# FFN of a hybrid decoder layer: the scales of a chunk's up and down weights from one chain, and the samples' parts of h from one instruction each

## The chip, the cores and the metric

The kernel runs on one core of one Trainium2 chip. The time is that of the device for one execution, in microseconds. The engines work side by side, each on its own queue in order: TensorE (PE, with its weight loads PEld), VectorE (DVE), ScalarE (ACT), GpSimd (POOL), and SyncE (SP), which here issues the DMA transfers.

## What is computed

One layer of a decoder trunk for 2048 prompt tokens and 32 sample tokens (8 samples of 4), width 1024. A mixing part (state space models, attention, a short convolution) comes first; the change leaves its instructions as they are. It is followed by the FFN:

```python
hn = rmsnorm(x, P['norm_ffn_g'][l])
x = x + jnp.square(jax.nn.relu(hn @ P['w_up'][l])) @ P['w_down'][l]
```

`w_up` is 1024 x 4096, `w_down` 4096 x 1024, all in float32; the prompt and the samples share the weights.

## The kernel before

**Numbers.** TensorE is fed with float16. Each float32 operand is split into a high part and a low part (`split`, L174: ScalarE writes the high part, VectorE the low one), and each product is made of three matmuls. So that weights fit the range of float16, a set of weights is multiplied by a power of two. `wscale` (L179) finds it: ScalarE squares the set and sums it by row (L183; the squares go to a junk place), a product with a matrix of ones sums over the partitions (through `mm`, L140), VectorE bounds it from below (L187), GpSimd raises it to the power -1/2 (L188), VectorE masks out the mantissa (`pow2`, L155), multiplies (L191) and takes the reciprocal (L192). This is a chain over four engines on a single column, 128 x 1.

**Tiling.** The FFN's width of 4096 is cut into 16 chunks of 256 columns (`FC`). The prompt is worked in two passes, s = 0 and s = 1, of two blocks of 512 tokens; the samples ride along with the first block of pass 0, so that its up products have 272 columns where the others have 256. In each pass all 16 chunks are loaded (1 MB of `w_up`, 1 MB of `w_down`) and split again. The scales are found in pass 0 alone and kept in `wsc` for pass 1.

**Both products use seven products for eight** (a Strassen-like scheme): GpSimd makes sums and differences of quarters of the up weights (L2036 to L2039), of the down weights (L2062 to L2065) and of h (L2138 to L2149). Chunk 15 takes the plain eight-product form for the down product.

**One chunk.** `ffn_wu` (L2019) loads the up weights, finds their scale in pass 0, and writes the split weights `wu`. `ffn_wd` (L2044) does the same for the down weights and writes `wd` and `wdT`. `up` (L2079) makes h for one block: seven products, ScalarE and VectorE add them up in the tile `fr` (four quarters, `C`), ScalarE applies relu and square, and then h is split into `ht`. In the first block of pass 0 the 16 sample columns of each quarter are also split, into `hs` (L2128 on ScalarE, L2129 on VectorE): four copies and four subtractions a chunk. `down` (L2154) multiplies h with the down weights and adds the result to the residual `x` (L2191, VectorE, one addition of 512 columns for each step); the samples' product comes first, 32 matmuls into a bank of its own, added to `accs` (L2166).

**The loop** (L2222 on) goes through steps (s, c, b), and each step issues in the program: `up` of the next step, then the weights of the next chunk (`ffn_wu` in the first block's step, `ffn_wd` in the second's), then `down` of this step.

**What sets the order.** The program order gives each instruction a priority; a planner in the tile framework, with a model of the engines' times, puts the instructions on the engines' queues and adds the waits. It takes a ready instruction of lower priority where one of higher priority isn't ready. So up and down products are interleaved on TensorE, and a change in one place can shift the planned order around it.

**Buffers.** The loaded weights (`ws`) have two buffers, used in turn by up and down weights: a load of down weights starts when the split of the chunk before has read the down weights for the last time (the wdT split, L177). `wu` has two buffers, `wd` and `wdT` share four. In PSUM, the tag `w` of the ones product uses the single bank `d`, which the samples' product uses too; down products and most of the up products rotate through five banks `b`, which come free when VectorE or ScalarE has read them.

Of the kernel before, what the change touches and what calls it, by code (L numbers as in the profile page):

```python
# [99 lines left out]
def dram(ap, offset, dims):  # L100
    return bass.AP(tensor=ap.tensor, offset=ap.offset + offset, ap=[list(d) for d in dims])


class K:
# [58 lines left out]
    def wprep(self, loads, kt, ncols, tag="w", st=None):  # L163


        nc = self.nc
        st = self.wload(loads, kt, ncols, tag) if st is None else st
        w = self.wp.tile([128, kt, 2, ncols], F16, name="w", tag=tag, bufs=None if tag == "w" else 1)
        sc, inv = self.col("w_sc", bufs=12), self.col("w_inv", bufs=12)
        self.wscale(st, w[:, :, 0, :], sc, inv, 15)  # L170
        self.split(w[:, :, 0, :], w[:, :, 1, :], st, sc)
        return w, sc, inv
# [5 lines left out]

    def wscale(self, st, junk, sc, inv, top):  # L179

        nc = self.nc
        ss = self.col("w_ss", bufs=4)
        nc.scalar.activation(junk, st, AF.Square, accum_out=ss)  # L183
        p = self.ps("w", [128, 512])
        self.mm(p[:, :1], self.ones, ss)
        f = self.col("w_f", bufs=4)
        nc.vector.tensor_scalar(f, p[:, :1], 1e-12, None, op0=OP.max)  # L187
        nc.gpsimd.tensor_tensor(f, f, self.mhalf[:, :1], op=OP.pow)  # L188
        m = self.col("w_m", bufs=4)
        self.pow2(m, f)  # L190
        nc.vector.tensor_scalar(sc, m, float(2 ** top), None, op0=OP.mult)  # L191
        nc.vector.reciprocal(inv, sc)  # L192
# [1684 lines left out]
    def outproj(self, ctx, mix):  # L1877
# [50 lines left out]
        self.accs = self.hp.tile([128, 8, NS], F32, name="accs")  # L1928
        self.wsc = self.hp.tile([128, 2, 4096 // FC, 2], F32, name="wsc")
        self.x2, self.hn = {}, {}  # L1930
# [52 lines left out]
    def out_sample(self, hn, g8):  # L1983
# [27 lines left out]
        for t in range(2):  # L2011
            for i in range(2):
                nc.vector.tensor_mul(xt[:, i, t], sq[:, :, 16 * t + 8 * i:16 * t + 8 * i + 8],
                                     g8[:, :, None].to_broadcast([128, 8, 8]))
# [28 lines left out]

    def ffn_wd(self, s, c):  # L2044


        nc, A = self.nc, self.A
        st = self.wload(lambda st: [(st, dram(A["w_down"], c * FC * D, [[D, 128], [128 * D, FC // 128], [1, D]]))], FC // 128, D)
        w = self.wp.tile([128, FC // 128, 2, D], F16, name="wd", tag="w")
        sc, inv = self.wsc[:, 1, c, 0:1], self.wsc[:, 1, c, 1:2]  # L2050
        if s == 0:
            self.wscale(st, w[:, :, 0, :], sc, inv, 14)
        if s == 0 or (s, c) in PLAIN:
# [16 lines left out]
    def ffn(self):  # L2070
# [8 lines left out]
        def up(s, c, b):  # L2079
# [29 lines left out]
            prod(r, 1, 1)  # L2109
            add(0, r, 0)  # L2110
            prod(p, 6, 3, False)
# [3 lines left out]
            prod(p, 4, 2, False)  # L2115
            nc.scalar.activation(C[:, 2, :], p[:, :N], AF.Relu, scale=RS)
            for i in range(4):
                x = C[:, i, :]
                if i != 2:
# [17 lines left out]
            A11, A22, A21, A12 = (C[:, i, :] for i in range(4))  # L2137
            nc.gpsimd.tensor_add(S[:, 0, :], A21, A22)  # L2138
# [6 lines left out]
            nc.scalar.activation(ht[:, 0:2, 0, :], C[:, 0:2, :], AF.Copy)  # L2145
            nc.gpsimd.tensor_sub(ht[:, 0:2, 1, :], C[:, 0:2, :], ht[:, 0:2, 0, :])  # L2146
            nc.scalar.activation(ht[:, 2, 0, :], A12, AF.Copy)
# [5 lines left out]
        def down(s, c, b, ht, f):  # L2153
# [26 lines left out]
        def down_pair(wd, wt, x2, ht, f):  # L2180
# [11 lines left out]
            p, q, r = (self.ps("mm", [128, 512]) for _ in range(3))  # L2192
            prod(p, 0, "11")
            add(0, 0, p)
# [5 lines left out]
            add(1, 0, p)  # L2200
            prod(q, 1, "T4", False)
            add(1, 0, q)
# [5 lines left out]
        def down_plain(wd, x2, ht, f):  # L2208
            for t, parts in enumerate(((0, 3), (2, 1))):
                for h in range(2):  # L2210
# [94 lines left out]
```

## Time and profile before

| what | value |
|---|---|
| median of 3 runs | 2594.95 us |
| lowest and highest | 2593.56 and 2594.98 us |
| profiled execution, its own time | 2598.28 us |
| span of that execution in the trace | 2596.5 us |
| TensorE busy | 2439.7 us (94%) |
| VectorE busy | 2010.8 us (77%) |
| ScalarE busy | 1313.2 us (51%) |
| GpSimd busy | 1212.3 us (47%) |

The FFN takes about the second half of the span: pass 0 from about 1300 us to 1957 us, pass 1 from there to the end. Busy shares are over the whole span; a stage has its own. The granted clock of TensorE is given as a share of full speed, and it is at full speed in the stretches shown below.

### The profile page before, as it was taken

Reading aid. Unit: us, or ns where it says so; the run is one execution under the profiler, and the core shown is the slowest. Engines: PE = TensorE matmul, PEld = TensorE weight load, DVE = VectorE, ACT = ScalarE, POOL = GpSimd, SP = SyncE. Lnnn points to the kernel's source line nnn. Section 1 sums busy time; section 2 is a strip of 40 time slices with the busy share of each in tenths; the row PEclk is TensorE's granted clock in tenths of the full one; section 3 lists DMA queues with packets and bytes.
Section 4 is the critical chain, followed back from the end, with each engine's and each line's share of the span. In section 5 each row is a group of like instructions: output and inputs, shape, how many; then the busy total and the mean of one; then the engine's idle time right before and its main releaser. Section 6 shows DMA issues by size and latency. Waiting matters only on the chain.

```text
span 2596.5 us, 51309 instructions
## 1 busy us (share of the span) xinstructions
PE 2439.7 (94%) x20496; PEld 1663.5 (64%) x20496; DVE 2010.8 (77%) x3746; ACT 1313.2 (51%) x2449; POOL 1212.3 (47%) x1265
## 2 busy tenths in 40 slices
PE   7989999999999899999979999999998999999997
PEld 6975554454467677689856666666665666666664
DVE  7566667874576777654589998889997898999996
ACT  6534332033346677562455555665556454555554
POOL 3403122223114566550255555656556665666652
PEclk9989999999999998999979999999999999999999
DMA  6333416879632433356111111111135211121201
GB/s 176 102 81 86 99 30 218 302 248 334 224 101 77 136 96 104 101 171 216 52 41 50 51 64 50 49 66 34 62 124 214 74 62 49 53 66 49 66 33 65
DMA packets 209321, 277.78 MB, mean 107 GB/s; under 512 B 42837, under 2 KB 177106, under 8 KB 198810
## 3 DMA queue, kind: packets, MB, share of 16 engines
q1 hardware_dynamic: 195050, 202.65, 25.0%
q0 software_dynamic: 9376, 67.64, 7.2%
q10 hardware_dynamic: 4656, 4.23, 0.5%
q8 instruction: 160, 2.62, 0.4%
q14 instruction: 79, 0.65, 0.1%
HBM read 217.33 MB, written 54.29 MB: 105 GB/s over the span
## 4 chain that ended last, share of the span: by engine, by line
PE 51%; DVE 16%; POOL 13%; DMA 6%; ACT 6%; issue 5%; SPq 1%; POOLq 0%; DVEq 0%; ACTq 0%
PE pb L140 25%; PE px L140 23%; DVE x L2191 4%; DVE wu L177 2%; PE pd L140 2%; DMA kp<-in_cache_v_dram,ptV 1%; DVE wd L177 1%; PE pb L144 1%; POOL ht L2146 1%; POOL ws L2037 1%; POOL ht L2148 1%; DVE wdT L177 1%; POOL ws L2039 1%; POOL ws L2038 1%; POOL ws L2036 1%
## 5 line engine op out<-in xcount | busy, mean ns | idle before, releaser
L140 PEld LDWEIGHTS <-wu 128*128 128x128 f16 x5376 | 530.3, 99 | 222.9 <-issue 37.3
L2191 DVE SCALAR_TENSOR_TENSOR x<-pb,ff,x 128x512 f32<-128x512 f32 x840 | 591.3, 740 | 27.3 <-PE pb L140 23.3
L140 PE MATMUL px<-hn,wu 128*128 128x256 f16 (+1 forms) x3072 | 428.0, 276 | 14.6 <-DVE hn L1981 7.0
L140 PEld LDWEIGHTS <-ht 128*128 128x128 f16 x2712 | 264.5, 99 | 231.6 <-issue 26.0
L140 PE MATMUL pb<-wdT,ht 128*128 128x512 f16 x1440 | 379.8, 381 | 15.8 <-DVE x L2191 9.2
L140 PE MATMUL px<-xT,w 128*128 128x512 f16 (+1 forms) x1968 | 371.9, 341 | 1.5 <-ACT da L731 1.2
L140 PE MATMUL pb<-wd,ht 128*128 128x512 f16 x1272 | 336.8, 381 | 6.1 <-DVE x L2191 5.2
L140 PE MATMUL pb<-hn,wu 128*128 128x256 f16 (+1 forms) x2304 | 303.6, 277 | 15.8 <-DVE x L2191 7.6
L140 PEld LDWEIGHTS <-w 128*128 128x128 f16 x2160 | 168.6, 99 | 188.1 <-issue 30.9
L909 POOL TENSOR_TENSOR pl<-P,ph 128x512 f16<-128x512 f32 (+3 forms) x160 | 166.9, 1053 | 155.5 <-ACT ph L906 59.6
L176 ACT ACTIVATE wu<-ws,wsc 128x1024 f16<-128x1024 f32 (+1 forms) x128 | 129.4, 1036 | 130.8 <-POOL ws L2039 76.7
L140 PE MATMUL px<-w,cat 128*128 128x256 f16 x1536 | 180.2, 274 | 3.4 <-DMA cat<-cat 3.3
L177 DVE SCALAR_TENSOR_TENSOR wu<-ws,wsc,wu 128x1024 f16<-128x1024 f32 (+1 forms) x128 | 168.6, 1331 | 18.0 <-ACT wu L176 17.7
L140 PEld LDWEIGHTS <-cat 128*128 128x128 f16 x1536 | 149.6, 98 | 25.7 <-DMA cat<-cat 3.4
L140 PE MATMUL px<-w,xT 128*128 128x128 f16 (+1 forms) x2400 | 156.1, 225 | 10.2 <-DVE v L576 4.5
L140 PEld LDWEIGHTS <-xT 128*128 128x128 f16 (+1 forms) x2672 | 153.1, 101 | 15.5 <-issue 5.5
L902 ACT ACTIVATE P<-pb,nck,cc 128x512 f32<-128x512 f32 (+3 forms) x160 | 112.2, 710 | 75.4 <-PE pb L140 69.7
L2143 ACT ACTIVATE ht<-fr 128x1024 f16<-128x1024 f32 (+1 forms) x60 | 64.2, 1070 | 159.9 <-POOL fr L2149 159.9
L2146 POOL TENSOR_TENSOR ht<-fr,ht 128x512 f16<-128x512 f32 (+1 forms) x60 | 84.2, 1403 | 113.0 <-ACT ht L2145 113.0
L2062 POOL TENSOR_TENSOR ws<-ws 128x512 f32<-128x512 f32 x30 | 41.1, 1371 | 187.1 <-DVE wd L177 187.1
L871 DVE TENSOR_REDUCE mx<-pb 128x1 f32<-128x512 f32 (+3 forms) x160 | 94.8, 607 | 40.0 <-PE pb L140 38.9
L2120 ACT ACTIVATE fr<-fr 128x256 f32<-128x256 f32 (+1 forms) x192 | 77.0, 414 | 90.5 <-DVE fr L2101 89.7
(717 smaller groups left out, 4647.1 us busy)
## 6 DMA issues: line engine op xcount, KB each, us to landing
ws<-in_w_up_dram SPq DMA_DIRECT2D x32, 1024.0 KB
ws<-in_w_down_dram SPq DMA_DIRECT2D x32, 1024.0 KB
ws<-in_w_in_dram SPq DMA_DIRECT2D x22, 512.0 KB
x<-in_x_prompt_dram SPq DMA_DIRECT2D x16, 512.0 KB
cat<-cat SPq DMA_DIRECT2D x32, 256.0 KB
x<-in_x_prompt_dram SPq DMA_DIRECT2D x8, 1024.0 KB
out_y_prompt_dram<-x SPq DMA_DIRECT2D x32, 256.0 KB
hnD<-hnr SPq DMA_DIRECT2D x4, 1792.0 KB
```

The costliest lines, as they stand in the source:

```text
L140: self.nc.tensor.matmul(out, lhsT, rhs, start=start, stop=stop, skip_group_check=True)
L144: self.nc.tensor.transpose(out, in_, self.ident[:n, :n])
L176: self.nc.scalar.activation(hi, x, AF.Copy, scale=sc)
L177: self.nc.vector.scalar_tensor_tensor(lo, x, sc, hi, op0=OP.mult, op1=OP.subtract)
L871: nc.vector.tensor_reduce(mx[:, ii, jb:jb + 1], s[:, :n], axis=AX.X, op=OP.max)
L902: nc.scalar.activation(P[:, :n], s[:, :n], AF.Exp, bias=nck[:, j, h, kt:kt + 1], scale=cc[:, h // 2:h // 2 + 1])
L909: (nc.gpsimd if 1 else nc.vector).tensor_sub(pl[:, :n], P[:, :n], ph[:, :n])
L2062: nc.gpsimd.tensor_sub(B11, B12, B11)
L2120: nc.scalar.activation(x, x, AF.Relu)
L2143: nc.scalar.activation(ht[:, o:o + m, 0, :], x, AF.Copy)
L2146: nc.gpsimd.tensor_sub(ht[:, 0:2, 1, :], C[:, 0:2, :], ht[:, 0:2, 0, :])
L2191: nc.vector.scalar_tensor_tensor(o, p, f, o, op0=OP.mult, op1=OP.add)
```

## The change

1. `wscale` takes a list of weight sets and works on as many columns. For chunks 1 to 15 in pass 0, `ffn_wu` now loads the down weights as well (`wd_load`, kept in `wst_down` until `ffn_wd` takes them), squares both sets, and one chain finds both scales on two columns. The two sets of squares go to different parts of the `wu` tile. Chunk 0 keeps two chains of one column. `wsc` has its axes in another order, so that the two scales of a chunk stand side by side.
2. The samples' columns of all four quarters of h are copied by one ScalarE instruction and subtracted by one VectorE instruction, into a tile `hs` with its axes in another order (parts, t, m, i, n). For this the quarters stand in another order in `C`, and what indexes them is changed with it: the additions, the order of squares, the operands of the down products, and the order of the samples' halves in `out_sample`.
3. The samples' product reads `hs` through an access pattern with more axes (runs of 16 columns), with the same number of matmuls and columns.

```diff
     def wscale(self, sts, sc, inv, top):
-        nc = self.nc
-        ss = self.col("w_ss", bufs=4)
-        nc.scalar.activation(junk, st, AF.Square, accum_out=ss)
+        nc, n = self.nc, len(sts)
+        ss = self.col(f"w_ss{n}", w=n, bufs=4)
+        for k, (st, junk) in enumerate(sts):
+            nc.scalar.activation(junk, st, AF.Square, accum_out=ss[:, k:k + 1])
         p = self.ps("w", [128, 512])
-        self.mm(p[:, :1], self.ones, ss)
-        f = self.col("w_f", bufs=4)
-        nc.vector.tensor_scalar(f, p[:, :1], 1e-12, None, op0=OP.max)
-        nc.gpsimd.tensor_tensor(f, f, self.mhalf[:, :1], op=OP.pow)
-        m = self.col("w_m", bufs=4)
+        self.mm(p[:, :n], self.ones, ss)
+        f = self.col(f"w_f{n}", w=n, bufs=4)
+        nc.vector.tensor_scalar(f, p[:, :n], 1e-12, None, op0=OP.max)
+        nc.gpsimd.tensor_tensor(f, f, self.mhalf[:, :n], op=OP.pow)
+        m = self.col(f"w_m{n}", w=n, bufs=4)
...
     def ffn_wu(self, s, c):
-        sc, inv = self.wsc[:, 0, c, 0:1], self.wsc[:, 0, c, 1:2]
+        sc, inv = self.wsc[:, c, 0, 0:1], self.wsc[:, c, 1, 0:1]
         if s == 0:
-            self.wscale(st, w[:, 3:7].rearrange("p o k a n -> p (o k a n)")[:, :KT * FC].rearrange("p (k n) -> p k n", n=FC),
-                        sc, inv, 14)
+            flat = w.rearrange("p o k a n -> p (o k a n)")
+            sts = [(st, flat[:, 3072:5120].rearrange("p (k n) -> p k n", n=FC))]
+            if c:
+                self.wst_down[c] = self.wd_load(c)
+                sts.append((self.wst_down[c], flat[:, 5120:7168].rearrange("p (k n) -> p k n", n=D)))
+            n = len(sts)
+            self.wscale(sts, self.wsc[:, c, 0, :n], self.wsc[:, c, 1, :n], 14)
...
+    def wd_load(self, c):
+        A = self.A["w_down"]
+        return self.wload(lambda st: [(st, dram(A, c * FC * D, [[D, 128], [128 * D, FC // 128], [1, D]]))], FC // 128, D)
+
     def ffn_wd(self, s, c):
-        st = self.wload(lambda st: [(st, dram(A["w_down"], c * FC * D, [[D, 128], [128 * D, FC // 128], [1, D]]))], FC // 128, D)
+        st = self.wst_down.pop(c, None) or self.wd_load(c)
         w = self.wp.tile([128, FC // 128, 2, D], F16, name="wd", tag="w")
-        if s == 0:
-            self.wscale(st, w[:, :, 0, :], sc, inv, 14)
+        if (s, c) == (0, 0):
+            self.wscale([(st, w[:, :, 0, :])], sc, inv, 14)
...
         def up(s, c, b):
...
                 hs = self.hp.tile([128, 2, 2, 2, 2, 8], F16, name="hs", bufs=2)
-                for m in range(2):
-                    for t in range(2):
-                        x = C[:, ((0, 2), (3, 1))[m][t], :].rearrange("p (i n) -> p i n", i=2)[:, :, 128:]
-                        nc.scalar.activation(hs[:, m, 0, t], x, AF.Copy)
-                        nc.vector.tensor_sub(hs[:, m, 1, t], x, hs[:, m, 0, t])
+                x = C.rearrange("p c (i n) -> p c i n", i=2)[:, :, :, 128:]
+                hh, hl = (hs[:, a].rearrange("p t m i n -> p (t m) i n") for a in range(2))
+                nc.scalar.activation(hh, x, AF.Copy)
+                nc.vector.tensor_sub(hl, x, hh)
...
         def down(s, c, b, ht, f):
...
-                        x, o = hs[:, k].rearrange("p a t i n -> p (a t i n)"), p[:, m].rearrange("p a n -> p (a n)")
+                        x, o = hs[:, :, :, k], p[:, m].rearrange("p a (t i n) -> p a t i n", t=2, i=2)
                         self.mm(o, wd[:, k, 0, m * 128:(m + 1) * 128], x, start=m + k == 0, stop=False)
-                        self.mm(o[:, 0:NS], wd[:, k, 1, m * 128:(m + 1) * 128], x[:, 0:NS], start=False, stop=k == 1)
+                        self.mm(o[:, 0], wd[:, k, 1, m * 128:(m + 1) * 128], x[:, 0], start=False, stop=k == 1)
```

## Rows read from the trace of the kernel before

**Rows 1.** the page's engine totals: busy us, share, instructions

```profile
PE 2439.7 (94%) x20496; PEld 1663.5 (64%) x20496; DVE 2010.8 (77%) x3746; ACT 1313.2 (51%) x2449; POOL 1212.3 (47%) x1265
```

**Rows 2.** engines by stretch, pass 0 then pass 1: us, busy per engine, clock, DMA

```profile
1410.24:1896.02 485.78, 466.61 (x3474) 312.63 (x3472) 440.64 (x711) 285.43 (x504) 282.73 (x265) 1.00 0.16 53
2203.35:2497.05 293.70, 293.57 (x2019) 197.30 (x2018) 276.54 (x366) 152.12 (x281) 186.78 (x162) 1.00 0.18 58
```

**Rows 3.** waits in pass 0 (1342 to 1957): total us, times, longest

```profile
PE pb L140 <- DVE x L2191: 20.2, 19, 4.4
DVE w_m L155 <- POOL w_f L188: 9.5, 9, 1.6
DVE hs L2129 <- ACT hs L2128: 6.8, 10, 3.3
```

**Rows 4.** timeline of a stall: start, us, engine, line, [idle <-releaser]

```profile
1610.01 2.35 DVE L177 SCALAR_TENSOR_TENSOR wdT<-ws,wsc,wdT 128x2048 f16<-128x2048 f32 x1 [0.41 <-ACT wdT L176]
1612.28 1.27 DVE L2129 TENSOR_TENSOR hs<-fr,hs 128x16 f16<-128x16 f32 x2
1614.13 0.73 DVE L2129 TENSOR_TENSOR hs<-fr,hs 128x16 f16<-128x16 f32 x1
1614.26 0.81 PE L140 MATMUL pb<-wdT,ht 128*128 128x512 f16 x3 [2.27 <-DVE x L2191]
```

**Rows 5.** VectorE's groups in pass 0: count, busy us, mean ns, idle before

```profile
L2129 DVE TENSOR_TENSOR hs<-fr,hs 128x16 f16<-128x16 f32 x60 | 32.5, 548 | 6.8 <-ACT hs L2128 6.8
L155 DVE TENSOR_SCALAR w_m<-w_f 128x1 int32<-128x1 int32 x29 | 4.2, 146 | 9.6 <-POOL w_f L188 9.5
```

**Rows 6.** timeline, an hs subtraction and the GpSimd operation before it

```profile
1525.93 1.26 POOL L2065 TENSOR_TENSOR ws<-ws 128x512 f32<-128x512 f32 x1
1526.10 1.13 DVE L2129 TENSOR_TENSOR hs<-fr,hs 128x16 f16<-128x16 f32 x1 [0.55 <-ACT hs L2128]
```

**Rows 7.** nearest sizes: VectorE's groups of the whole run; GpSimd's power on 32 columns

```profile
L1981 DVE TENSOR_TENSOR hn<-os,hn 128x128 f16<-128x128 f32 x2 | 0.5, 282 | 0.0
1260.52 5.82 POOL L2007 TENSOR_TENSOR os_rs<-os_rs,mhalf 128x32 f32<-128x32 f32 x1 [4.01 <-DVE os_rs L2006]
```

**Rows 8.** timeline, the sample product's first matmuls of that chunk

```profile
1623.41 0.92 PE L140 MATMUL pd<-hs,wd 128*128 128x64 f16 x28
```

**Rows 9.** timeline, loads, squares, ones products and scales of one chunk

```profile
1595.95 0.37 SPq L160 DMA_DIRECT2D ws<-in_w_up_dram  x1
1602.70 1.91 ACT L183 ACTIVATE wu<-ws 128x2048 f16<-128x2048 f32 x1 [3.83 <-DMA ws<-in_w_up_dram]
...
1611.71 0.28 PE L140 MATMUL pd<-w_ss,ones 128*128 128x1 f32 x2
1612.38 0.37 SPq L160 DMA_DIRECT2D ws<-in_w_down_dram  x1
1620.06 0.14 DVE L191 TENSOR_SCALAR wsc<-w_m 128x1 f32<-128x1 f32 x1
...
1632.52 0.37 SPq L160 DMA_DIRECT2D ws<-in_w_up_dram  x1
1633.23 0.28 PE L140 MATMUL pd<-w_ss,ones 128*128 128x1 f32 x2
1635.84 0.55 POOL L188 TENSOR_TENSOR w_f<-w_f,mhalf 128x1 f32<-128x1 f32 x1
1638.86 0.14 DVE L191 TENSOR_SCALAR wsc<-w_m 128x1 f32<-128x1 f32 x1
1640.21 1.99 ACT L176 ACTIVATE wd<-ws,wsc 128x2048 f16<-128x2048 f32 x1
...
1654.44 0.37 SPq L160 DMA_DIRECT2D ws<-in_w_down_dram  x1
```

**Rows 10.** timeline, chunk 1, both scales at hand together

```profile
1348.28 0.15 DVE L191 TENSOR_SCALAR wsc<-w_m 128x1 f32<-128x1 f32 x1
...
1372.35 0.37 SPq L160 DMA_DIRECT2D ws<-in_w_down_dram  x1
```

More of the change, by code (lines that the diff above doesn't have):

```diff
@@ L169, in wprep @@
         sc, inv = self.col("w_sc", bufs=12), self.col("w_inv", bufs=12)
-        self.wscale(st, w[:, :, 0, :], sc, inv, 15)
+        self.wscale([(st, w[:, :, 0, :])], sc, inv, 15)
         self.split(w[:, :, 0, :], w[:, :, 1, :], st, sc)
@@ L177, in split, with wscale @@
         self.nc.vector.scalar_tensor_tensor(lo, x, sc, hi, op0=OP.mult, op1=OP.subtract)
-    def wscale(self, st, junk, sc, inv, top):
-        nc = self.nc
-        ss = self.col("w_ss", bufs=4)
-        nc.scalar.activation(junk, st, AF.Square, accum_out=ss)
-        p = self.ps("w", [128, 512])
-        self.mm(p[:, :1], self.ones, ss)
-        f = self.col("w_f", bufs=4)
-        nc.vector.tensor_scalar(f, p[:, :1], 1e-12, None, op0=OP.max)
-        nc.gpsimd.tensor_tensor(f, f, self.mhalf[:, :1], op=OP.pow)
-        m = self.col("w_m", bufs=4)
+    def wscale(self, sts, sc, inv, top):
+        nc, n = self.nc, len(sts)
+        ss = self.col(f"w_ss{n}", w=n, bufs=4)
+        for k, (st, junk) in enumerate(sts):
+            nc.scalar.activation(junk, st, AF.Square, accum_out=ss[:, k:k + 1])
+        p = self.ps("w", [128, 512])
+        self.mm(p[:, :n], self.ones, ss)
[3 more added lines that the diff above has]
+        m = self.col(f"w_m{n}", w=n, bufs=4)
         self.pow2(m, f)
@@ L1928, in outproj @@
         self.accs = self.hp.tile([128, 8, NS], F32, name="accs")
-        self.wsc = self.hp.tile([128, 2, 4096 // FC, 2], F32, name="wsc")
+        self.wsc = self.hp.tile([128, 4096 // FC, 2, 2], F32, name="wsc")
+        self.wst_down = {}
         self.x2, self.hn = {}, {}
@@ L2012, in out_sample @@
             for i in range(2):
-                nc.vector.tensor_mul(xt[:, i, t], sq[:, :, 16 * t + 8 * i:16 * t + 8 * i + 8],
+                nc.vector.tensor_mul(xt[:, i, 1 - t], sq[:, :, 16 * t + 8 * i:16 * t + 8 * i + 8],
                                      g8[:, :, None].to_broadcast([128, 8, 8]))
@@ L2042, in ffn_wu @@
         self.wts[s, c] = w, inv
+    def wd_load(self, c):
+        A = self.A["w_down"]
+        return self.wload(lambda st: [(st, dram(A, c * FC * D, [[D, 128], [128 * D, FC // 128], [1, D]]))], FC // 128, D)
     def ffn_wd(self, s, c):
-        nc, A = self.nc, self.A
-        st = self.wload(lambda st: [(st, dram(A["w_down"], c * FC * D, [[D, 128], [128 * D, FC // 128], [1, D]]))], FC // 128, D)
+        nc = self.nc
+        st = self.wst_down.pop(c, None) or self.wd_load(c)
         w = self.wp.tile([128, FC // 128, 2, D], F16, name="wd", tag="w")
-        sc, inv = self.wsc[:, 1, c, 0:1], self.wsc[:, 1, c, 1:2]
-        if s == 0:
-            self.wscale(st, w[:, :, 0, :], sc, inv, 14)
+        sc, inv = self.wsc[:, c, 0, 1:2], self.wsc[:, c, 1, 1:2]
+        if (s, c) == (0, 0):
+            self.wscale([(st, w[:, :, 0, :])], sc, inv, 14)
         if s == 0 or (s, c) in PLAIN:
@@ L2109, in up @@
             prod(r, 1, 1)
-            add(0, r, 0)
+            add(2, r, 0)
             prod(p, 6, 3, False)
@@ L2115, in up @@
             prod(p, 4, 2, False)
-            nc.scalar.activation(C[:, 2, :], p[:, :N], AF.Relu, scale=RS)
-            for i in range(4):
+            nc.scalar.activation(C[:, 0, :], p[:, :N], AF.Relu, scale=RS)
+            for i in (2, 1, 0, 3):
                 x = C[:, i, :]
-                if i != 2:
+                if i:
                     nc.scalar.activation(x, x, AF.Relu)
@@ L2136, in up @@
                 return ht, hs
-            A11, A22, A21, A12 = (C[:, i, :] for i in range(4))
+            A21, A22, A11, A12 = (C[:, i, :] for i in range(4))
             nc.gpsimd.tensor_add(S[:, 0, :], A21, A22)
@@ L2144, in parts @@
                 nc.vector.tensor_sub(ht[:, o:o + m, 1, :], x, ht[:, o:o + m, 0, :])
-            nc.scalar.activation(ht[:, 0:2, 0, :], C[:, 0:2, :], AF.Copy)
-            nc.gpsimd.tensor_sub(ht[:, 0:2, 1, :], C[:, 0:2, :], ht[:, 0:2, 0, :])
+            nc.scalar.activation(ht[:, 0:2, 0, :], C[:, 1:3, :], AF.Copy)
+            nc.gpsimd.tensor_sub(ht[:, 0:2, 1, :], C[:, 1:3, :], ht[:, 0:2, 0, :])
             nc.scalar.activation(ht[:, 2, 0, :], A12, AF.Copy)
@@ L2192, in down_pair @@
             p, q, r = (self.ps("mm", [128, 512]) for _ in range(3))
-            prod(p, 0, "11")
+            prod(p, 1, "11")
             add(0, 0, p)
@@ L2200, in down_pair @@
             add(1, 0, p)
-            prod(q, 1, "T4", False)
+            prod(q, 0, "T4", False)
             add(1, 0, q)
@@ L2208, in down_plain @@
         def down_plain(wd, x2, ht, f):
-            for t, parts in enumerate(((0, 3), (2, 1))):
+            for t, parts in enumerate(((2, 3), (0, 1))):
                 for h in range(2):
```

## The prediction

> **What bounds the kernel now.** I read first the page's engine totals: TensorE is busy 94% of the span [rows 1], so the change can only pay where TensorE stands still, or where it removes TensorE work. Then I cut the span by stage. The change touches only pass 0 of the FFN (scales are found there alone, and only its first block carries the samples), so I compared a steady stretch of pass 0 with one of pass 1 [rows 2]. The first holds 12 chunks in 485.78 us, 40.48 us each; the second, eight chunks in 293.70 us, 36.71 us each. In pass 1 TensorE never stops (293.57 of 293.70 busy), though VectorE is busy 94% there. In pass 0 TensorE is busy 38.88 us of each 40.48 and VectorE 91%. So VectorE's load alone does not stall TensorE; something in pass 0 makes it late at the wrong moments. About 15 chunks run like this, so TensorE's idle time there is some 15 x 1.60 = 24 us, and that is nearly all there is to win.
>
> The view of waits says who ends that idle time: 20.2 us of it is a down product waiting for VectorE to add an earlier one to the residual (L2191), so that a PSUM bank comes free [rows 3]. The timeline of one such place shows why VectorE was late [rows 4]: it finished the 2.35 us split of wdT, then did two of the small subtractions for hs (1.27 us for both), and only then the addition that let TensorE go on after 2.27 us; the next thing on VectorE was another hs, 0.73 us. I went through all stalls of this kind: in 14 of the 19, together 18 us, an hs subtraction stands within the few VectorE instructions just ahead.
>
> **The change part by part.**
> *The samples' parts.* Four subtractions per chunk become one. There are 60 in the FFN of pass 0, 548 ns in the mean for 16 columns [rows 5]. That price is not their work. The rows show the reason: a subtraction that began at 1526.10 while GpSimd was inside an operation ended at 1527.23, and that operation ended at 1527.19 [rows 6]. The work alone is small: a subtraction of 128 columns took 282 ns [rows 7]. The merged one has 64 columns, so it should take under 282 ns unblocked, and once in a while a GpSimd operation more; I take the same 548 ns. VectorE then loses 45 x 0.548 = 24.7 us of busy time and about three quarters of the 6.8 us it waits for ScalarE's copies [rows 3]. If the price went instead with the columns, one merged subtraction would cost 4 x 0.548 = 2.2 us and nothing would be saved; against that stands that subtractions of the same 16 columns took 0.73 us at one place [rows 4] and 1.13 us at another [rows 6]. The Trainium skill ("SBUF — State Buffer", Who interferes with whom) says that a VectorE instruction with two SBUF inputs and a GpSimd instruction that reads SBUF exclude each other for the whole of the earlier one; by that rule too the price is paid per instruction, and the saving is the 24.7 us, not zero. ScalarE's four copies become one; it is busy 59% of this stretch [rows 2] and this costs or gives nothing on the path. The merged pair must wait for the last of the four quarters of h. Its reader, the sample product, needs all four today too, and came at 1623.41 [rows 8], 8.5 us after the hs subtraction that began at 1614.13 had ended [rows 4]; that gap hides the wait. Were it gone, at most the price of one subtraction, 0.7 us there, would be added in each chunk.
>
> What reaches TensorE: of the 18 us of stalls with an hs subtraction ahead, I take half, 9 us. The reason for half is that a typical stall has one or two of these in the queue ahead (0.55 to 1.3 us), and its mean is 18/14 = 1.3 us, the rest being the wdT split and the additions. Bounds 0 and 18 us.
>
> *One chain instead of two.* For chunks 1 to 15 one of the two chains of ones product, max, power, mask, multiplication and reciprocal goes. On TensorE that is two passes, 0.28 us in the timeline [rows 9], 15 x 0.28 = 4.2 us; this lies on the engine that sets the end, so it counts in full. On VectorE four operations of about 146 ns [rows 5] go, 15 x 0.58 = 8.8 us, and about half of the 9.5 us that it waits for GpSimd's power [rows 3]. The power itself takes 5.82 us for 32 columns [rows 7] against 0.55 us for one (1635.84, [rows 9]), about 170 ns a column, so the two-column one costs about 0.72 us, less than two. I give VectorE's relief here no price of its own beyond the 9 us above; with it, at most all of the 24 us idle time goes.
>
> *The new wait.* The scale of the up weights now also needs the down weights' load and its sum of squares. Program order puts that load just behind the up load on SP's queue; both are already issued when their buffer comes free, in turn, so the queue itself gains nothing behind it. What waits is the chain. Today in one chunk [rows 9]: the down load is issued at 1612.38 (its buffer is read for the last time by the wdT split), the ones product of the up weights has just run at 1611.71, and their scale is there at 1620.06, 7.7 us after the down load's issue. A load takes about 6.7 us (issued 1595.95, ScalarE's square started at 1602.70 having waited 3.83 us for it), the square 1.9 us, the accumulator read 0.2 us; from ones product to scale there are 5.6 us (1633.23 to 1638.86) or 8.4 us (1611.71 to 1620.06). So the common scale comes 14.4 to 17.2 us after the down load's issue, the up weights are split 7 to 10 us later than now, but the down weights' scale comes some 9 to 12 us earlier than its 1638.86. While it waits, the square holds up ScalarE's copies out of PSUM, and the ones product holds up every product queued behind it on TensorE.
>
> Is that covered? The down buffer makes a loop: load, square, chain, splits of both, next load. Chunk 1 is the nearest row for the splits with both scales at hand: from the first of the two scales at 1348.28 to the next down load at 1372.35, 24.1 us [rows 10]. With 24.1 the loop is 14.4 + 24.1 = 38.5 us at the better chain, 41.3 us at the worse. TensorE's own work will be 38.88 - 0.28 = 38.6 us a chunk. So the loop lies just at TensorE's floor at the better end and passes today's 40.48 us at the worse. I take it as covered, at no cost, because the up split's late start is followed by an early down split, and TensorE has both blocks' down products to do meanwhile; but with no room to spare.
>
> **Sum.** 4.2 + 9 = 13 us off the profiled execution's 2598.28 us (span 2596.5 and 1.8 around it), 2585 us. The median of the three runs is 3.3 us lower, 2594.95, so I forecast 2594.95 - 13 = 2582, and say 2581 for the small gains not counted. All of TensorE's idle time gone would be 4.2 + 24 = 28 us, 2567.
>
> **The rivals.**
> *The loop paces pass 0* (slower). If the planned order lets the down weights' split start only after the last part of the up weights', the two follow each other: 12.3 us for up (1620.2 to 1632.5) and 14.2 us for down (1640.21 to 1654.44), 26.5 us [rows 9]. With 14.4 to 17.2 us ahead of it the period is 40.9 to 43.7 us against 40.48; in the middle 42.3, 15 x 1.8 = 27 us slower, 2622 (from 2601 to 2643). It decides from a period of 40.5 us on. For it: in the chunk of [rows 9] the down split does stand behind the up split, and in the chunks before and after it as well. Against it: there it waited for its own scale, which now comes with the other, and chunk 1 interleaved them. Chance 0.23.
> *The relief is hidden.* TensorE's waits end at L2191 for other reasons, the wdT split and the additions; only the 4.2 us of ones products count: 2591. Against it: hs in 14 of 19 stalls. Chance 0.17.
> *The sample product gets slower.* Its moving operand is now read in runs of 16 columns. There are 512 such products; 28 of them took 0.92 us in one merged row of the timeline [rows 8], at most 33 ns each. If that doubled, some 17 us would be added and the gain lost: 2599. No row shows a moving operand in such short runs; bounds are nothing and this. I take nothing, as the up product's operand in two runs keeps its rate. Chance 0.04.
> Forecast as summed: 0.56.
>
> **How the numbers follow.** Faster by over 0.2% (5.2 us, about what a measurement of this kernel can tell from no change): the forecast, 0.56. Within 0.2%: the two cases in the middle with the rounding, 0.19. Slower: the loop with a little for a replanned order elsewhere, 0.25. The range must leave out 0.2 at most: downward it goes to all idle time gone, 2566; upward it takes in the lower part of the loop's case, to 2608. The forecast's own range is 2567 to 2590.
>
> **What would show it.** In the changed kernel's trace: hs subtractions 16 instead of 64, and two-column sums; the wait of TensorE for L2191 near 11 us instead of 20; chunks of pass 0 about 39.6 us apart, counted between down loads; pass 1 unchanged at 36.7. Wrong, and the loop right, if TensorE or ScalarE waits for the down load through the ones product or the square, with the down loads over 40.5 us apart. Wrong, and the relief hidden, if the hs rows fall as foreseen and the waits for L2191 stay at 20 us.

## The result and the profile after

The changed kernel takes 2618.82 us (median of 4 runs, 2615.38 to 2620.66) against 2594.26 us before: ratio 1.0094, 95% interval 1.0077 to 1.0112. It is slower by 24.6 us, outside the forecast range of 2566 to 2608, and on the side of the first rival, whose price was 2622 us.

The page's head and engine totals of the changed kernel:

```profile
span 2618.2 us, 51067 instructions
PE 2437.4 (93%) x20466; PEld 1659.7 (63%) x20466; DVE 1996.2 (76%) x3638; ACT 1307.4 (50%) x2401; POOL 1216.3 (46%) x1250
```

Every engine but GpSimd is busy for less time than in [rows 1], and the span is longer. In all that follows I compare two stretches per kernel, cut at down loads: ten chunks of pass 0 (from the fifth down load to the fifteenth) and seven of pass 1. Each row gives the stretch, its length, then busy time and count of TensorE, weight loads, VectorE, ScalarE and GpSimd, then the granted clock and the DMA share. First the same cut of the kernel before, whose stretches in [rows 2] are a little longer, then the changed kernel:

```profile
1450.86:1855.95 405.09, 385.99 (x2867) 258.06 (x2867) 366.57 (x592) 237.23 (x420) 236.39 (x222) 1.00 0.16 53
2203.35:2460.38 257.03, 256.90 (x1767) 172.67 (x1766) 243.12 (x323) 133.18 (x246) 163.47 (x142) 1.00 0.18 58
```
```profile
1450.14:1873.89 423.75, 391.69 (x2879) 259.67 (x2877) 358.90 (x523) 235.35 (x391) 239.78 (x210) 0.99 0.16 51
2225.36:2482.05 256.69, 256.69 (x1766) 172.53 (x1765) 242.77 (x323) 132.71 (x245) 163.00 (x141) 1.00 0.18 58
```

Pass 1 is what it was, 36.7 us a chunk. Pass 0 went from 40.51 to 42.38 us a chunk, although VectorE's busy time fell by 7.7 us. From the first down load to the seventeenth (the first of pass 1) it is 652.96 us before (1273.21 to 1926.17) and 676.48 us after (1270.48 to 1946.96): 23.5 us more, the whole loss.

One chunk of the changed kernel, from a down load to the next (timeline; start, duration, engine, line, operation):

```profile
1705.39 0.37 SPq L160 DMA_DIRECT2D ws<-in_w_down_dram  x1
1710.22 1.91 ACT L185 ACTIVATE wu<-ws 128x2048 f16<-128x2048 f32 x1 [0.79 <-DMA ws<-in_w_down_dram]
...
1714.69 0.28 PE L140 MATMUL pd<-w_ss,ones 128*128 128x2 f32 x2
...
1714.79 0.23 DVE L2141 TENSOR_TENSOR hs<-fr,hs 128x64 f16<-128x64 f32 x1 [2.17 <-ACT hs L2140]
...
1721.25 0.16 DVE L193 TENSOR_SCALAR wsc<-w_m 128x2 f32<-128x2 f32 x1
1721.45 1.76 ACT L176 ACTIVATE wu<-ws,wsc 128x1024 f16<-128x1024 f32 x2 [2.09 <-DVE wsc L193]
1723.12 1.99 ACT L176 ACTIVATE wd<-ws,wsc 128x2048 f16<-128x2048 f32 x1
...
1731.11 1.27 POOL L2047 TENSOR_TENSOR ws<-ws 128x512 f32<-128x512 f32 x1
...
1732.33 2.26 POOL L2074 TENSOR_TENSOR ws<-ws 128x512 f32<-128x512 f32 x1
...
1741.80 1.26 POOL L2077 TENSOR_TENSOR ws<-ws 128x512 f32<-128x512 f32 x1
...
1743.10 2.00 ACT L176 ACTIVATE wdT<-ws,wsc 128x2048 f16<-128x2048 f32 x1 [3.47 <-POOL ws L2077]
1745.14 2.35 DVE L177 SCALAR_TENSOR_TENSOR wdT<-ws,wsc,wdT 128x2048 f16<-128x2048 f32 x1 [2.91 <-ACT wdT L176]
1747.52 0.37 SPq L160 DMA_DIRECT2D ws<-in_w_down_dram  x1
```

The common scale comes 15.9 us after the down load's issue (1721.25), and 26.3 us later the down buffer has been read for the last time: 42.1 us, and the next four chunks repeat it to a tenth of a microsecond. The same places in [rows 9] are a chunk of 42.1 us too, but one of chunks that vary around 40.5 us, with the up scale 7.7 us after the down load.

The waits of pass 0 (total us, times, longest) in the changed kernel, against [rows 3]:

```profile
PE pb L140 <- DVE x L2203: 36.9, 27, 2.4
DVE hs L2141 <- ACT hs L2140: 28.1, 14, 2.9
ACT wu L185 <- DMA ws<-in_w_down_dram: 11.3, 13, 1.7
```

TensorE's wait for the additions to the residual was to fall from 20.2 to 11 us; it rose to 36.9. VectorE stands 28.1 us in front of the merged subtraction, about 2 us each time: in the chunk above, ScalarE's copy for it comes behind the down square, which had waited for the load, and behind some operations on h that follow the square. So there were two suspects, the coupled scales and the merged subtraction, and the experiments begin by parting them.

### The profile page after: what moved, and what is told of

Same layout as the page of the kernel before. It is cut to its first block, busy times and chain, and to the rows that moved or that the text cites. A ratio compares the mean times of both kernels' runs of the same rounds, so it can differ in the third digit from the quotient of the medians.

```text
span 2618.2 us, 51067 instructions
## 1 busy us (share of the span) xinstructions
PE 2437.4 (93%) x20466; PEld 1659.7 (63%) x20466; DVE 1996.2 (76%) x3638; ACT 1307.4 (50%) x2401; POOL 1216.3 (46%) x1250
## 4 chain that ended last, share of the span: by engine, by line
PE 58%; DVE 13%; POOL 12%; DMA 6%; ACT 5%; issue 4%; SPq 1%; POOLq 0%; DVEq 0%; ACTq 0%
PE pb L140 29%; PE px L140 25%; DVE x L2203 2%; PE pd L140 2%; DVE wu L177 2%; DMA ws<-in_w_down_dram 1%; DMA kp<-in_cache_v_dram,ptV 1%; DVE wdT L177 1%; PE pb L144 1%; POOL ws L2046 1%; ACT wdT L176 1%; POOL ws L2075 1%; POOL ws L2045 1%; POOL ws L2074 1%; POOL ws L2047 1%
## 5 line engine op out<-in xcount | busy, mean ns | idle before, releaser
L2203 DVE SCALAR_TENSOR_TENSOR x<-pb,ff,x 128x512 f32<-128x512 f32 x840 | 589.0, 741 | 28.7 <-PE pb L140 26.3
L140 PE MATMUL pb<-hn,wu 128*128 128x256 f16 (+1 forms) x2304 | 297.8, 275 | 6.6 <-ACT fr L2110 2.7
L2158 POOL TENSOR_TENSOR ht<-fr,ht 128x512 f16<-128x512 f32 (+1 forms) x60 | 75.1, 1251 | 225.4 <-ACT ht L2157 217.3
L2132 ACT ACTIVATE fr<-fr 128x256 f32<-128x256 f32 (+1 forms) x192 | 77.4, 414 | 100.6 <-DVE fr L2113 100.4
L2133 ACT ACTIVATE fr<-fr 128x256 f32<-128x256 f32 (+1 forms) x256 | 101.8, 412 | 3.8
```

The source lines that it names most:

```text
L140: self.nc.tensor.matmul(out, lhsT, rhs, start=start, stop=stop, skip_group_check=True)
L2158: nc.gpsimd.tensor_sub(ht[:, 0:2, 1, :], C[:, 1:3, :], ht[:, 0:2, 0, :])
L2203: nc.vector.scalar_tensor_tensor(o, p, f, o, op0=OP.mult, op1=OP.add)
```

## The experiments

**One part at a time.** e_hs is the kernel before with the samples' part of the change alone, e_scales the one with the scales' part alone.

```diff
-                for m in range(2):
-                    for t in range(2):
...
+                x = C.rearrange("p c (i n) -> p c i n", i=2)[:, :, :, 128:]
+                hh, hl = (hs[:, a].rearrange("p t m i n -> p (t m) i n") for a in range(2))
+                nc.scalar.activation(hh, x, AF.Copy)
+                nc.vector.tensor_sub(hl, x, hh)
```

> Only the samples' part of the change: one copy and one subtraction for hs, scales found in two chains as before. If the loop of the down weights' buffer (load, square, common chain, both splits, next load) paces the changed kernel, it is absent here: chunks of pass 0 some 39.6 to 40.4 us apart, 2576 to 2594 us. If instead the merged subtraction is what costs (VectorE stands 28.1 us in the changed kernel's trace waiting for the merged copy), this kernel is as slow as the changed one, 2610 to 2625 us.

```diff
+            if c:
+                self.wst_down[c] = self.wd_load(c)
+                sts.append((self.wst_down[c], flat[:, 5120:7168].rearrange("p (k n) -> p k n", n=D)))
+            n = len(sts)
+            self.wscale(sts, self.wsc[:, c, 0, :n], self.wsc[:, c, 1, :n], 14)
```

> Only the scales' part of the change: one chain on two columns, hs in four copies and four subtractions as before. Loop theory: chunks of pass 0 at least 42 us apart, 2612 to 2640 us. Theory of the merged subtraction: 2580 to 2597 us.

Measured: e_hs 2620.58 us, ratio 1.0109 (1.0091 to 1.0127); e_scales 2614.49 us, ratio 1.0085 (1.0067 to 1.0104). Each part alone is as slow as both together. The whole times would have convicted both; the stretches part them. e_hs, then e_scales:

```profile
1447.66:1844.46 396.80, 384.78 (x2863) 258.67 (x2861) 350.38 (x558) 232.23 (x387) 233.81 (x219) 0.99 0.16 54
2198.10:2484.02 285.92, 264.09 (x1766) 174.94 (x1765) 255.15 (x323) 134.69 (x245) 175.19 (x141) 0.98 0.16 52
```
```profile
1446.83:1869.36 422.53, 391.27 (x2860) 257.23 (x2860) 364.07 (x552) 242.07 (x423) 237.09 (x210) 0.99 0.15 51
2220.89:2477.57 256.68, 256.68 (x1766) 172.50 (x1765) 242.75 (x323) 132.71 (x245) 163.05 (x141) 1.00 0.18 58
```

In e_hs pass 0 is faster than before, 39.68 us a chunk instead of 40.51, and pass 1, whose work the samples don't touch, goes at 40.85 us instead of 36.7. In e_scales pass 0 alone is slow, 42.25 us, as in the changed kernel. The same work of pass 1 (1766 matmuls in each of these rows) in 29 us more: that is another planned order of the same instructions, and a later run tests it. Of these 29 us, 21.8 are TensorE standing still, and 7.4 are a longer busy time for the same matmuls, at a granted clock of 0.98 instead of 1.00. Also in e_hs, the two rows that the prediction had named (the wait of TensorE; VectorE's group of subtractions):

```profile
PE pb L140 <- DVE x L2191: 11.5, 15, 1.7
```
```profile
L2129 DVE TENSOR_TENSOR hs<-fr,hs 128x64 f16<-128x64 f32 x15 | 7.1, 472 | 0.0
```

**The same kernel without the wait.** e_nowait keeps every instruction of the changed kernel; only the source of the second sum of squares is the up weights again. Each scale's reciprocal is applied to the products afterwards, so which power of two is taken drops out of the outputs. (The expectation below says that the outputs change by a power of two; that is wrong.)

```diff
-                sts.append((self.wst_down[c], flat[:, 5120:7168].rearrange("p (k n) -> p k n", n=D)))
+                sts.append((st, flat[:, 5120:7168].rearrange("p (k n) -> p k n", n=FC)))
```

> The changed kernel, but the second sum of squares is taken from the up weights again instead of the down weights, so the number and size of the instructions stay and the chain no longer waits for the down weights' load (the down weights' scales, and with them the FFN's outputs, are then another power of two). Loop theory: the loop loses load and square, 6.8 us, so it no longer paces: chunks 38.6 to 40 us apart, 2565 to 2592 us. If the cost is elsewhere (merged subtraction, a planned order that is worse as such): 2610 us or more.

Measured: 2568.53 us, ratio 0.991 (0.9893 to 0.9926). Its two stretches:

```profile
1430.29:1821.74 391.45, 382.45 (x2848) 256.13 (x2847) 353.89 (x521) 232.54 (x388) 228.37 (x210) 1.00 0.17 55
2172.85:2429.52 256.67, 256.67 (x1766) 172.49 (x1765) 242.74 (x323) 132.64 (x245) 163.01 (x141) 1.00 0.18 58
```

Taking away that one dependence is worth 50 us against the changed kernel: 39.15 us a chunk instead of 42.38, and TensorE idle 0.9 us a chunk instead of 3.2 (span less busy, a tenth of the row's difference). The edit also takes away the wait of ScalarE's second square for the load; the next kernel keeps that wait.

**Two chains in the new place.** e_two has the loads and both squares where the changed kernel has them, but a chain for each.

```diff
-            self.wscale(sts, self.wsc[:, c, 0, :n], self.wsc[:, c, 1, :n], 14)
+            for k, one in enumerate(sts):
+                self.wscale([one], self.wsc[:, c, 0, k:k + 1], self.wsc[:, c, 1, k:k + 1], 14)
```

> The changed kernel with both sums of squares and both loads at the changed place in the program, but two chains of one column, so that the up weights' scale waits only for the up weights. Loop theory (the shared chain couples both): pass 0 within 5 us of the kernel with merged hs and two chains in the old place (651 us from first down load to the seventeenth), far under the changed kernel's 676. If the early place of the down load and square is what costs: 670 to 680. The order of instructions in pass 1 is the one that went with 603 us for pass 1, so the whole is 2612 to 2625 us under the loop theory and 2640 or more under the other.

Measured: 2638.99 us, ratio 1.0181 (1.0152 to 1.0211). The two stretches:

```profile
1444.81:1843.63 398.82, 386.75 (x2863) 258.38 (x2861) 357.01 (x557) 232.75 (x390) 226.54 (x219) 0.99 0.16 54
2212.37:2496.87 284.50, 261.80 (x1739) 171.79 (x1737) 255.81 (x321) 133.60 (x243) 173.45 (x140) 0.98 0.16 53
```

Pass 0 is 39.88 us a chunk, 651.0 us from first down load to seventeenth, as foreseen: not the place of the load and the square, but that one chain serves both, costs the time. The whole lies 14 us over the 2625 that went with this outcome, and a microsecond under the 2640 of the other, because pass 1 took 621 us in a slower order where I had reckoned with 603; by the whole time alone I would have taken the wrong side.

**A longer load.** In pass 0 the down weights are loaded twice into the same buffer, in the changed kernel and in the kernel before.

```diff
-    def wd_load(self, c):
+    def wd_load(self, c, s=0):
...
-        return self.wload(lambda st: [(st, dram(A, ...))], FC // 128, D)
+        return self.wload(lambda st: [(st, dram(A, ...)) for _ in range(2 if s == 0 else 1)], FC // 128, D)
```

> The changed kernel with the down weights of pass 0 loaded twice into the same buffer. Loop theory: what the second MB adds to the time from issue to landing (3 to 6 us) is added to each of 14 periods, 2655 to 2705 us. If the loop does not pace, the longer load is covered: 2615 to 2630 us.

> The kernel before with the down weights of pass 0 loaded twice into the same buffer, the control for the same step in the changed kernel, which added 49 us to pass 0. If the kernel before has slack in its down loop, pass 0 grows by less than 10 us (653 to 663). If any longer load costs the same, it grows by 40 us or more.

Measured: 2695.39 us, ratio 1.0397 (1.0375 to 1.0419), for the changed kernel; 2588.72 us, ratio 0.9995 (0.9979 to 1.0011), for the kernel before. From the load's issue to the square that waits for it, first in the changed kernel, then in the kernel before:

```profile
1725.92 5.78 SPq L160 DMA_DIRECT2D ws<-in_w_down_dram  x2
1736.25 1.91 ACT L185 ACTIVATE wu<-ws 128x2048 f16<-128x2048 f32 x1 [2.25 <-DMA ws<-in_w_down_dram]
```
```profile
1646.52 5.20 SPq L160 DMA_DIRECT2D ws<-in_w_down_dram  x2
1656.23 1.91 ACT L183 ACTIVATE wd<-ws 128x2048 f16<-128x2048 f32 x1 [1.13 <-DMA ws<-in_w_down_dram]
```

In both the data are there after about 10 us; with one load the square of the changed kernel started after 4.8. The ten chunks of pass 0, first in the changed kernel, then in the kernel before:

```profile
1448.05:1904.55 456.50, 406.06 (x2871) 262.65 (x2869) 372.22 (x524) 235.68 (x391) 251.22 (x210) 0.96 0.21 70
1441.46:1850.27 408.81, 391.72 (x2885) 261.50 (x2884) 373.16 (x591) 237.06 (x420) 240.43 (x221) 0.98 0.24 78
```

The kernel before hides the longer load: 40.88 us a chunk, 0.37 more than without; from the first down load to the seventeenth it is 662.03 us, 9 more, just within the bound. Its trace shows why: with a single load, ScalarE comes to the down square only 7.3 to 10.2 us after the issue, having other work before it, so a load of 10 us delays the square by some 1.5 us and not by 5. The changed kernel pays 3.3 of some 5 us in every chunk, 45.65 each. Of these 32.75 us in ten chunks, 18.4 are TensorE standing still and 14.4 a longer busy time, at a granted clock of 0.96 instead of 0.99. (About 33 us of its loss are in pass 1, which again has a slower order: 604.65 us between the same loads, against 571.75.)

**Shortening the loop.** If one loop of fixed length paced pass 0, any microsecond taken out of it would come back, down to TensorE's floor. Three kernels try that. e_early gives the chain an earlier priority in chunks 0 to 13 (chunk 0 is in it too, though the expectation says 1 to 13); e_first puts the down split ahead of the up split; e_noB leaves out GpSimd's four differences of the down weights in pass 0, and e_noB_before leaves them out of the kernel before, by the same edit.

```diff
+            with self.priority(self.tc.cur_priority - (300 if c < 14 else 0)):
-            self.wscale(sts, self.wsc[:, c, 0, :n], self.wsc[:, c, 1, :n], 14)
+                self.wscale(sts, self.wsc[:, c, 0, :n], self.wsc[:, c, 1, :n], 14)
```

> The changed kernel with its common chain, from the squares to the reciprocal, given a priority 300 instructions earlier for chunks 1 to 13. In the changed kernel's trace the chain spends some 7 us of its loop queued behind other work (ones product 2.5 us after the square's end, max 1.9 us later, multiplication 2.5 us after the mask). If the loop paces and these are part of it, chunks fall from 42.4 towards TensorE's floor, 39.2 to 40.5 us, and with pass 1 in the order of the before kernel the whole is 2570 to 2592 us. If the chain's place in the queues doesn't matter, 2610 to 2620 us.

```diff
+            if c:
+                self.wts[s, c] = ()
+                self.ffn_wd(s, c)
         A11, A21, A12, A22 = (st[:, 4 * k:4 * k + 4, 128 * m:128 * m + 128] for k in range(2) for m in range(2))
...
```

> The changed kernel with the down weights' split placed before that of the up weights, right behind the common chain. If the loop is that of the down weights' buffer alone, its splits shrink from 26 to about 15 us and the loop to some 31 us, so TensorE paces: 39 to 40 us a chunk, pass 0 at 630 to 645. If the common chain makes a loop of whichever buffer is read last, the up weights take the place of the down weights and chunks stay 40.5 to 43.5 us apart, pass 0 at 655 to 690. Pass 1 has the order of the before kernel, about 571 us.

```diff
-        nc.gpsimd.tensor_sub(B11, B12, B11)
-        nc.gpsimd.tensor_sub(B12, B22, B12)
-        nc.gpsimd.tensor_sub(B22, B22, B11)
-        nc.gpsimd.tensor_sub(B21, B21, B22)
+        if s:
+            nc.gpsimd.tensor_sub(B11, B12, B11)
...
```

> The changed kernel without GpSimd's four differences of the down weights in pass 0 (the down products of pass 0 are then made of the wrong quarters). In the changed kernel the down buffer's loop passes through them: the first starts 11.1 us after the common scale, the last ends 10.7 us later. If that loop paces, taking them out brings the down load forward and chunks of pass 0 fall from 42.4 to TensorE's floor, 39 to 40 us. If the up weights' half of the cycle is as long (scale, four sums, last split, load, square, chain), the gain stops early, 41 us or more. Pass 1 has one of the slower planned orders, so the whole time says little; the chunks of pass 0 count.

> The same four differences left out of the kernel before, as a control (the down products of pass 0 are then made of the wrong quarters). If no loop paces there, its chunks fall by less than 1 us, to 39.5 to 40.5 us; a fall as large as in the changed kernel would mean that GpSimd's work itself is the cost in both.

Measured: e_early 2604.89 us, ratio 1.0051 (1.0035 to 1.0067); e_first 2649.52 us, ratio 1.0222 (1.0188 to 1.0257); e_noB 2636.53 and e_noB_before 2616.06 us beside 2591.18, a single run each, both with a slower order of pass 1 (283.01 and 286.85 us for seven chunks). The ten chunks of pass 0 in e_early, e_first, e_noB and e_noB_before:

```profile
1445.63:1864.94 419.31, 390.33 (x2876) 258.99 (x2876) 364.26 (x523) 234.80 (x393) 231.52 (x210) 1.00 0.16 51
1453.65:1908.52 454.87, 401.71 (x2886) 260.02 (x2884) 373.58 (x522) 240.51 (x391) 238.46 (x210) 0.98 0.14 46
1425.56:1835.66 410.10, 389.01 (x2877) 257.97 (x2878) 356.63 (x523) 234.89 (x390) 211.91 (x172) 1.00 0.16 53
1436.42:1836.14 399.72, 383.49 (x2861) 257.44 (x2860) 366.45 (x589) 235.74 (x420) 169.52 (x180) 1.00 0.17 54
```

That is 41.93, 45.49, 41.01 and 39.97 us a chunk. A down load, the square, the ones product where it is shown, the scale and the next down load, in e_early and in e_noB:

```profile
1698.27 0.37 SPq L160 DMA_DIRECT2D ws<-in_w_down_dram  x1
1703.12 1.91 ACT L185 ACTIVATE wu<-ws 128x2048 f16<-128x2048 f32 x1 [0.61 <-DMA ws<-in_w_down_dram]
...
1711.05 0.15 DVE L193 TENSOR_SCALAR wsc<-w_m 128x2 f32<-128x2 f32 x1
...
1740.40 0.37 SPq L160 DMA_DIRECT2D ws<-in_w_down_dram  x1
```
```profile
1711.26 0.37 SPq L160 DMA_DIRECT2D ws<-in_w_down_dram  x1
1717.94 1.91 ACT L185 ACTIVATE wu<-ws 128x2048 f16<-128x2048 f32 x1 [1.14 <-DMA ws<-in_w_down_dram]
...
1730.85 0.28 PE L140 MATMUL pd<-w_ss,ones 128*128 128x2 f32 x2
...
1734.44 0.16 DVE L193 TENSOR_SCALAR wsc<-w_m 128x2 f32<-128x2 f32 x1
...
1754.24 0.37 SPq L160 DMA_DIRECT2D ws<-in_w_down_dram  x1
```

In this chunk of e_early the scale is there after 12.8 us instead of 15.9, and the splits then take 29.4 us instead of 26.3: the 3.1 us were given back inside the chunk. In this chunk of e_noB the splits take 19.8 us, but the ones product now stands 11 us behind the end of the square, with other products ahead of it on TensorE, and the scale comes after 23.2 us. It is one of two kinds: chunks of about 43 us alternate with chunks of 38.4 to 40.4, whose scale comes after 19 to 20.3 us. The gain over the changed kernel is 1.4 us a chunk, 0.5 of which the control has as well. e_early met neither of its two cases: the chunks did not fall to 40.5 us, and the whole lies between the bounds. e_noB, at 41.01 us, stands at the edge of its second case (41 or more), and its control met its bounds. e_first went further to the slow side than foreseen (732 us from the first down load to the seventeenth, 690 at most expected). So the picture of one loop of fixed links falls. What stands is that the cycle with the common chain stretches when a link gets longer, and hardly shrinks when one gets shorter, because other links grow in its place; that the planner's order does this is my reading and is not tested. Which link holds it near 41 to 42 us in these cases is open. The planned order of pass 0 differs from kernel to kernel, so one could suspect that the changed kernel merely had a bad one. Against that stands the whole set: the six kernels in which one chain waits for both loads (the changed one, e_scales, e_load2_after, e_early, e_first, e_noB) take 41.0 to 45.7 us a chunk, the eight others (before, e_hs, e_nowait, e_two, e_load2_before, e_noB_before, e_hs8, e_lean) 39.2 to 40.9.

**The order of pass 1.** e_hs8 is e_hs with the four-part split kept for chunks 8 to 15. Nothing in pass 1 differs between the two in instructions; the planned orders do. Cut at the wdT splits, VectorE's order in pass 1 repeats one block from some chunk on in the kernel before, the changed kernel, e_scales, e_nowait and e_hs8, and goes through other blocks in e_hs, e_two and e_load2_after. The traces of the other kernels sort the same way: that one block repeats in e_load2_before, e_early, e_first and e_lean too, and not in e_noB and e_noB_before.

```diff
-                nc.scalar.activation(hh, x, AF.Copy)
-                nc.vector.tensor_sub(hl, x, hh)
+                for q in ([slice(0, 4)] if c < 8 else [slice(j, j + 1) for j in (2, 0, 3, 1)]):
+                    nc.scalar.activation(hh[:, q], x[:, q], AF.Copy)
+                    nc.vector.tensor_sub(hl[:, q], x[:, q], hh[:, q])
```

> Two chains as before; hs in one copy and one subtraction for chunks 0 to 7, in four and four for chunks 8 to 15. Its planned order in pass 1 repeats the same block as that of the before kernel, where the kernel with hs merged in all chunks repeats another. If that kernel's loss of 28 us is the order of pass 1: pass 1 here 566 to 575 us, pass 0 within 5 us of 652, whole 2583 to 2597 us. If merged subtractions slow pass 1 through something else, half of the loss stays: 2605 or more.

Measured: 2585.9 us, ratio 0.9984 (0.9969 to 1.0000); its stretch of pass 1:

```profile
2192.42:2449.06 256.64, 256.64 (x1766) 172.57 (x1765) 242.72 (x323) 132.64 (x245) 163.00 (x141) 1.00 0.18 58
```

36.66 us a chunk, and the whole is 35 us under e_hs. (Between loads, pass 0 is 658.7 and pass 1 557.5 us, not in the bounds I gave; the load that I take as their border came later here. Their sum, 1216.3, is 38 us under e_hs's 1254.2.) So e_hs lost its time through the planner's order in pass 1, not through the merged subtraction.

**A version faster than both.** e_lean drops the down weights' sum of squares for chunks 1 to 15 and takes both scales from the up weights' sum.

```diff
-                sts.append((self.wst_down[c], flat[:, 5120:7168].rearrange("p (k n) -> p k n", n=D)))
...
-        sc, inv = self.wsc[:, c, 0, 1:2], self.wsc[:, c, 1, 1:2]
+        sc, inv = (self.wsc[:, c, a, 0 if c else 1:1 if c else 2] for a in range(2))
```

> The changed kernel with no sum of squares of the down weights for chunks 1 to 15: both scales are taken from the up weights' sum, on one column. Less work than the kernel whose second sum was taken from the up weights (2568.5 us): 15 squares fewer on ScalarE and a one-column chain. If TensorE paces that kernel already, 2560 to 2570 us; if ScalarE's squares still delayed something there, down to 2550.

Measured: 2574.62 us, ratio 0.992 (0.9903 to 0.9937), over both bounds of the expectation. The ten chunks of pass 0:

```profile
1432.87:1830.42 397.55, 387.42 (x2895) 260.03 (x2894) 349.48 (x522) 220.02 (x372) 231.34 (x211) 1.00 0.16 54
```

It is not faster than e_nowait: 15 squares fewer on ScalarE buy nothing that shows. TensorE stands still for only 1.0 us a chunk here (0.9 in e_nowait), so little was left to win. Both versions rest on the down weights being of about the size of the up weights; with weights of another range a scale of their own would be needed.

## Why the prediction was wrong

*What bounds the kernel.* Right. TensorE's idle time in pass 0 was all there was to win, and e_nowait won most of it: 24 us, where all of it gone was put at 28.

*The samples' parts: mechanism right, size about right.* In e_hs the merged subtraction takes 472 ns for 64 columns where one of 16 took 548 [rows 5], so the price is per instruction; the group falls from 32.5 to 7.1 us. TensorE's wait for L2191 falls from 20.2 us to 11.5, forecast 11. Over the ten chunks pass 0 gains 0.83 us a chunk, which would be 12 us in 15 chunks, where 9 were counted; but from the first down load to the seventeenth it is 651.16 us against 652.96, only 1.8 less, so the size depends on where the stretch is cut. The half of 18 us was a choice between wide bounds, and that the wait came out so near is in part luck. In the changed kernel none of this shows (42.38 us a chunk against 42.25 in e_scales).

*One chain instead of two: not isolated.* I counted 4.2 us. e_nowait against e_two, one chain of two columns against two of one, both in the new place, differ by 0.73 us a chunk, 11 us; but e_nowait's second scale and square also don't wait for the down load, and the planned orders differ, so no run shows what the missing chain alone is worth.

*The new wait: the step that failed.* "I take it as covered, at no cost." It cost 3.2 us a chunk (42.38 against 39.15 without it; 2.5 against e_two's 39.88, which has the second chain to pay for), 48 us over 15 chunks, which ate the gains of both parts and 24 us more. The working had the parts: 14.4 to 17.2 us from the down load to the common scale (measured 15.9), and 24.1 us from chunk 1 [rows 10] or 26.5 us from the serial splits [rows 9] to the next load (measured 26.3). The first sum came out right with two errors that offset each other: the down load was taken at the 6.7 us of an up load and took 4.8, and the ones product, for which no wait was counted, stood 2.5 us behind the end of the square. Of the four sums, 38.5 to 43.7, three lay over today's 40.48 us, and I took the one that didn't: the shorter chain together with the splits of chunk 1. In that chunk of the kernel before, the down split went first on ScalarE, and GpSimd was done with the down weights' differences (L2065) before the last sum of the up weights (L2039):

```profile
1350.22 1.99 ACT L176 ACTIVATE wd<-ws,wsc 128x2048 f16<-128x2048 f32 x1
1352.11 1.75 ACT L176 ACTIVATE wu<-ws,wsc 128x1024 f16<-128x1024 f32 x2
...
1365.12 1.27 POOL L2065 TENSOR_TENSOR ws<-ws 128x512 f32<-128x512 f32 x1
...
1367.70 2.14 POOL L2039 TENSOR_TENSOR ws<-ws 128x512 f32<-128x512 f32 x1
```

The changed kernel's chunk above has it the other way round. The reason given for the cover, down products for TensorE to do meanwhile, hides a delay, but not a period: what comes 42 us after its predecessor in every chunk is not caught up by other work.

*The rival.* Its price, 42.3 us a chunk and 2622 us, was met (42.16 us over the last six of the ten chunks, 2618.8 us); and so was the sign named for it: ScalarE's square waits 11.3 us for the down load. Its condition was met in part. On ScalarE the down split began right behind the first parts of the up split (1723.12). But its second half, wdT, needs GpSimd's four differences of the down weights, and these begin at 1732.33, as the last sum of the up weights (L2047) ends; among operations on h they run to 1743. And as e_early and e_noB show, it is no fixed loop, and the order alone does not cure it: e_first, with the down split first, is slower still.

*The sample product.* No slower: 33 ns a matmul, as in [rows 8].

```profile
1723.95 0.90 PE L140 MATMUL pd<-hs,wd 128*128 128x64 f16 x27
```

*Pass 1* stayed at 36.7 us, as forecast, but not for a reason I had: the planned order there could have gone the other way, as it did in e_hs, at a cost of 35 us against e_hs8.

*Range and chances.* The range ended at 2608 with a rival of chance 0.23 centred on 2622; its upper end cut that case rather than holding it.

## What to carry to other kernels

Before two chains are merged into one, write down when each one's inputs arrive and when each one's result is needed: the merged one has the later arrival for both, and if the result frees the buffer whose next load is that arrival, the delay recurs in every turn. Here other work did not hide it. When a bound is a sum of ranges, and most combinations lie on one side of the point that decides, forecast that side. Where a planner orders the instructions, compare stages, not whole times: two edits here, e_hs and e_two, would have been judged wrongly by their totals.

## What the runs showed that I had not expected

The same instructions of pass 1 settle into one of several planned orders: 36.7 us a chunk in the nine kernels that repeat the one block, 40.1 to 41.0 us in the five others (e_hs 40.85, e_two 40.64, e_load2_after 40.11, e_noB 40.43, e_noB_before 40.98). These instructions being the same, what leads into one or the other is presumably where the plan of pass 0 leaves off; how it does is not shown. In the slow ones TensorE is busy 92 to 93% of the stretch, in the fast one all of it. That alone is worth 30 to 50 us here, as much as the largest effect of an edit in this study.
